# Four of the sixteen gates computed as two Strassen pairs inside the values' stage

## The chip, the core and the metric

The kernel runs on one core of a Trainium2 chip. The metric is the device time of one execution in microseconds (us). TensorE is called PE here, VectorE DVE, ScalarE ACT, GpSimd POOL and SyncE SP. Besides PE, an execution keeps DVE and ACT busy with element work, and SP and POOL with issuing transfers.

## What is computed

One decoder layer, batch 1, 1024 tokens, 1024 channels, float32. Only the first half matters here.

```
h   = rms_norm(x)
q,k,v (attention A: 4 heads, causal, two softmaxes), q,k,v (attention B: 3 dilated groups x 4 heads), 2 x 1024 gate columns = h @ w_in
yA  = DiffAttn(h) @ W_A_out ; yB = DilatedMix(h) @ W_B_out
x   = x + rms_norm((sigmoid(gA) * yA + sigmoid(gB) * yB) @ W_mix_out)
x   = x + rms_norm(ConvGLU(rms_norm(x)))
```

## The kernel before

**Matmuls in three products.** Every float32 operand is split into a rounded high half and the low rest (`whi`/`wlo`, `xh`/`xl`, and so on; `split`, lines 149 on ACT and 146 on DVE). `mm3` makes a product from three matmuls, high by high, high by low and low by high (lines 155, 156 and 157). A matmul with 512 moving columns is the unit in which most of the work comes.

**The values' stage.** After the start, all value columns of both attentions (4 blocks of 512 columns in two halves `i` = 0 and 1) are computed by Strassen's scheme: seven products `p1` to `p7` in place of eight, over sums of blocks of the normalized input (`t2`, `t3`, `t4` and the blocks `b11` to `b22`) and sums of blocks of the weight. The table `steps_v` names the product and the k block of each step, and the loop over it fetches raw weights ahead (SP's queue, `load_raw`), makes the weight sums on DVE (line 345, tiles `wz` and `raw`), splits them (`ready_v`, tiles `whi` and `wlo`), multiplies (`step_v`), and takes sums out of PSUM (`take_v`, `put_v`; tiles `yv` to DRAM `v_d`). Work on tables (`sin`, `cos`, `rstd_row`) stands among these steps on DVE and ACT by the step numbers `NORM_AT` to `STORE_AT`.

**Gates.** Sixteen blocks of 128 gate columns (`proj_t`, 48 matmuls of 512 columns each) give `gt_d` in DRAM. `START_GATES`, `A_FILLS` and `B_GATES` say where they stand: one before attention A, twelve spread as fills among the attention jobs of its heads, three in attention B's last step.

**Attention and its fills.** `interleave` writes out the order: attention jobs (scores `s`, softmax in `bs` and `stat`, transposes `pt`, product `o`, sum `osb`) with "fills" between them, projections and gates, so that PE has work while DVE and ACT do a job's softmax. In `A_FILLS` one string per head of attention A lists the fills: `p` projects the next head, `v` and `w` fetch and split values, `g` is a gate, `P` projects the first head of attention B, `x` and `V` fetch and split its values. In attention B each step's fills are the projections of the next step (`acc` is their PSUM tile, `kh`, `kl`, `qh`, `ql` what they become after the rotation, tiles `t1` and `t2`). The framework's scheduler then fixes each engine's order; how far the projections run ahead of the jobs follows from it. Each engine works through its own order in sequence. PSUM holds one `o` tile for the second attention's jobs, so a job's first product waits until `osb` has taken the previous one out (ACT line 1027 copies, DVE line 1028 adds).

**The last attention step and behind it.** Head 3 of the last group runs with the gates as fills and, behind them, the products of attention A's output (`oah`, `oal`). What its groups gave is stored (`og_d`, `st_d`), weighed, read back and summed (`merge`: DVE lines 1107 to 1110, tiles `mw`, `og`, `om`), split to `obh` and `obl`, and multiplied (`acc2`, `acc`).

Of the kernel before, what the change touches and what calls it, by code (L numbers as in the profile page):

```python
# [15 lines left out]
F32 = mybir.dt.float32  # L16
F32R = mybir.dt.float32r
I32 = mybir.dt.int32
AF = mybir.ActivationFunctionType
ALU = mybir.AluOpType  # L20
# [4 lines left out]
P = 128  # L25
S = 1024
D = 1024
KC = D // P
# [18 lines left out]
NH = NF // 2  # L47
AHEAD, T1_AT, LAST = 4, 5, 7
MIX_UNITS = {3: (0,), 4: (1,), 5: (2, 4), 6: (5,), 7: (6, 3, 7)}
START_GATES, A_FILLS, B_GATES = 1, ("gpgg", "gpvgg", "wgpgg", "xgPVgg"), 3  # L50
SLOTS = 18
LEFT_PAD = 48


XT_BUFS, NORM_AT, ANGLES_AT, SINES_AT, TABLES_AT, STORE_AT = 6, 14, 25, 33, 34, {35: 0, 36: 3, 39: 2, 41: 1}

K_FIRST = (4, 0, 5, 1, 6, 2, 7, 3)
RSQRT_MAGIC = float(0x5F3759DF)
# [29 lines left out]
def trunk(ctx: ExitStack, tc: tile.TileContext, a, out):  # L88
    nc = tc.nc
# [17 lines left out]
    def psum(dt=F32, pool=acc, tag="acc"):  # L107
        return pool.tile([P, 512], dt, tag=tag, name=tag)
# [8 lines left out]
    def load_raw(src, tag="raw", width=512, parts=1):  # L117
        raw = (raws_in[-1].tile([P, 512], F32, tag=tag, name="raw") if isinstance(tag, str) else tag)[:, :width]
        if src is None:
            return raw  # L120
        if parts > 1:
            for c in range(0, width, width // parts):
                dma(raw[:, c : c + width // parts], src[:, c : c + width // parts])
            return raw
        to = raw if src.dtype == F32 else raw.bitcast(I32)
        dma(to if len(src.shape) == 2 else to.rearrange("p (b c) -> p b c", c=src.shape[-1]), src)
        return raw
# [20 lines left out]
    def split(hi, lo, src, eng=None):  # L148
        copy = nc.scalar.activation(hi, src, AF.Copy)  # L149
        sub(eng or nc.vector, lo, src, hi)  # L150
        return copy.ins
# [48 lines left out]
    def halves():  # L200
        return [slice(i * 512, (i + 1) * 512) for i in range(2)]
# [142 lines left out]
    def tt(o, x, y, op=ALU.subtract):  # L344
        nc.vector.tensor_tensor(o, x, y, op=op)  # L345
# [82 lines left out]
    def turn_norms():  # L428
        spread = rstd_row.rearrange("p (m q) -> p m q", q=P)
        nc.vector.tensor_copy(spread, rstd.unsqueeze(2).to_broadcast([P, 8, P]))  # L430
        for half, sl in enumerate(halves()):
            row = psum(F32, ps_s, "s")
            for b in range(4):
                nc.tensor.transpose(row[:, b * P : (b + 1) * P], spread[:, half * 4 + b], ident)
            nc.scalar.activation(rstd_row[:, sl], row, AF.Copy)
# [25 lines left out]
    with ExitStack() as st_y:  # L461
# [6 lines left out]
        def turns(pattern, *ps):  # L468

            ks = [iter(range(4)) for _ in ps]  # L470
            return [(ps[c], 1, next(ks[c])) for c in pattern]

        steps_v += [("p1", 1, k) for k in range(4)] + turns((0, 0, 1, 0, 1, 0, 1, 1), "p5", "p6")
        steps_v += turns((0, 0, 1, 1, 1, 1, 0, 0), "p3", "p7") + [("p4", 1, k) for k in range(4)]
        wz = [t[:, k % 2] for t in [wv.tile([P, 2, 512], F32, tag=f"wz{i}", name="wz") for i in range(2)] for k in range(2)]
        ready, got_v = {}, {}
# [10 lines left out]
        def new_y(name, pool=None):  # L487
            return [(pool or yv).tile([P, 512], F32, tag=f"y{name}{m}", name="yv") for m in range(4)]

        def fetch_v(n):  # L490
            p, i, k = steps_v[n]
            which = {"p1": ((0, 0),), "p2": ((0, 1),), "p5": ((1, 0), (1, 1)), "p6": ((0, 0),), "p7": ((0, 0), (1, 0)),
                     "p4": ((1, 1),), "p3": ((0, 1),)}[p]
            got_v[n] = [load_raw(a["w_v"][j * 4 + k][:, (2 * i + c) * 512 : (2 * i + c + 1) * 512], next(tags), parts=1 if n else 2)
                        for c, j in which]

        def ready_v(n, w=512):
            p, _, k = steps_v[n]
# [54 lines left out]
        quarter = {(0, i): new_y(f"a{i}") for i in range(2)}  # L553
        banks = {}

        def step_v(n):
            p, i, k = steps_v[n]
            x = xs_of[p]
            if p in ("p1", "p2", "p5") and k == 0:
                left = p == "p1"  # L560
                banks[left] = ([psum() for _ in range(3)] + [psum(F32, ps_o, "o")] if left else
                               [psum(F32, q, t) for q, t in ((ps_s, "s"), (pt, "pt")) for _ in range(2)])
            use = banks[p in ("p1", "p6", "p7", "p4")]
            wh, wl = ready.pop(n)
            for m in range(4):
                tk = slice(m * P, (m + 1) * P)
                mm3(use[m], x[0][:, k, tk], x[1][:, k, tk], wh, wl, k == 0 and p in ("p1", "p2", "p5"), k == 3, p in ("p6", "p7", "p4", "p3"))
            if k < 3:
                return
            with tc.high_priority(offset=80):  # L570
                for m in range(4):
                    take_v(p, i, m, use[m])
            if p == "p7" and i == 0:
                for m in range(4):
                    tt(quarter[3, 0][m], banks[False][m], quarter[3, 0][m], ALU.add)
# [56 lines left out]
        for n in range(8, len(steps_v)):  # L632
            p, i, k = steps_v[n]
            while fetched < min(n + (8 if n <= TABLES_AT else 10), len(steps_v)):
                fetch_v(fetched)
                fetched += 1
            while made < min(n + 5, len(steps_v)):
                ready_v(made)
                made += 1
            if 0 <= n - NORM_AT < 11:  # L640
                norm_x(n - NORM_AT)
            if n == NORM_AT + 11:
                lambda_scale()
            if n == TABLES_AT + 2:
                scale_tables(*args)
            if n == TABLES_AT + 4:
                tags = more_tags()
            if n == ANGLES_AT:
                pos = [load_raw(a["positions"][sl].partition_broadcast(P), next(tags)) for sl in halves()]
                args = [tb.tile([P, S], F32, tag=n_, name=n_) for n_ in ("sin", "cos")]  # L650
                angles(pos, *args, tb)
            if n in STORE_AT:
                put_v(STORE_AT[n], 0, True)
            if n == SINES_AT:
                make_sines(*args)
            if n == TABLES_AT:
                turn_norms()
            if k == 0 and (p, i) in places_y:
                q, name, pool = places_y[p, i]
                quarter[q, i] = new_y(name, pool)  # L660
            step_v(n)
            if k == 3 and i and p in ("p1", "p7", "p4", "p3"):
                put_v({"p1": 0, "p7": 3, "p4": 2, "p3": 1}[p], 1, p == "p1")
            if (p, i) == ("p5", 1):

                again.append(load_raw(a["xT"][k][:, 512:], next(tags)))
            if (p, i) == ("p6", 1):
                with behind_marks():
                    split_x(k, halves()[1], again[k])
# [15 lines left out]
                dma(v.rearrange("p (r ih) c -> p r ih c", ih=n)[:, :, ih], src[:, i * 4 // n : (i + 1) * 4 // n, ih])  # L685
        return vs

    def split_values(vs, res):

        with behind_marks():  # L690
            for v in vs:
                res.append(v_tiles())
                split(*res[-1], v)

    def rotated(ps, cos, sin, sl, quarter):
        t1 = rt.tile([P, 512], F32, tag="t1", name="t1")
# [172 lines left out]
        later(1, sums)  # L869
        later(3, norm)  # L870

    free_gates = list(range(2 * KC))

    def gates(n):

# [32 lines left out]
    def once(fn):  # L908

        fn()  # L910
        yield 0
# [13 lines left out]
    with st_a:  # L925
        ops = [[] for _ in range(AH)]
        vs = [[] for _ in range(AH // 2)]
        run(gates(START_GATES)[0])
        run(proj_a(0, ops[0]))
        split_values(fetch_values(1, 0), vs[0])  # L930
        of_pair = []
        for h in range(AH):
            out_sb, pair = {}, []
            todo = [functools.partial(attend_a, h, i, ops[h], vs[h // 2], out_sb, pair) for i in (6, 7, 4, 5, 2, 3, 0, 1)]
            kinds = {
                "p": lambda: (proj_a(h + 1, ops[h + 1]), 8),
                "v": lambda: (once(lambda: of_pair.extend(fetch_values(1, 256))), 0),
                "w": lambda: (once(lambda: split_values(of_pair, vs[1])), 0),
                "g": lambda: gates(1),
                "P": lambda: (proj_b(0, 0, ops_b[steps[0]]), 8),  # L940
                "x": lambda: (once(lambda: fetch_b(0, 0)), 0),
                "V": lambda: (once(lambda: split_b(0, 0)), 0),
            }
            if h + 1 == AH:
                tabs_b += load_tabs(0, 64)
            fills = [kinds[c]() for c in A_FILLS[h]]
            if h + 1 < AH:
                interleave(jobs(todo, a_weight), 52, *fills)
            else:
                interleave(itertools.chain(jobs(todo, a_weight), rest_due(12)), 64, *fills)  # L950
# [516 lines left out]
    def put(step, *srcs):  # L1467

        operands[step] = []
        for src in srcs:  # L1470
            operands[step].append(next(places)())
            split(*operands[step][-1], src)
# [329 lines left out]
```

## Time and profile before

| | |
|---|---|
| median of 3 runs | 1685.25 us (1685.08 to 1686.24) |
| profiled execution | 1684.85 us, its span 1683.1 us |
| granted PE clock | 0.999 |
| PE busy | 1668.5 us, 99% of the span |
| DVE busy | 1308.4 us, 78% |
| ACT busy | 913.4 us, 54% |
| POOL busy | 170.2 us, 10% |

The span runs from the first to the last instruction; 1.75 us of the execution lie outside it. "Busy" of PE is the union of pipelined matmuls, so an individual duration of some 390 ns is not its cost: consecutive matmuls start 0.227 us apart. Which stage binds on what has to be read by windows of time and by the waits.

### The profile page before, as it was taken

The page shows a single profiled execution, that of the slowest core. Times are in us where ns is not written, and L with a number is a line of the kernel's source. Part 1 is how long each engine was busy: PE and PEld are TensorE (multiplying, and loading weights), DVE is VectorE, ACT ScalarE, POOL GpSimd, SP SyncE. Part 2 cuts the span into 40 slices and gives each one's busy share as a digit, 9 for nine tenths or more (in the row PEclk, how much of TensorE's full clock was granted, in tenths as well). Part 3 has the DMA queues.
Part 4 walks back from the last instruction along what each step waited for, and adds up shares of the span by engine and source line. Part 5 has one row for each costly group of instructions (what it writes and reads, how often), then busy time and mean ns, then how long its engine had stood idle before and what let it go on. Part 6 is the DMA issues. An engine that isn't in the chain of part 4 may idle for free. (4 is left out here: it accounts for less than half of the span.)

```text
span 1683.1 us, 22937 instructions
## 1 busy us (share of the span) xinstructions
PE 1668.5 (99%) x7878; PEld 1394.0 (83%) x7878; DVE 1308.4 (78%) x2430; ACT 913.4 (54%) x1707; POOL 170.2 (10%) x267
## 2 busy tenths in 40 slices
PE   9999999999999999999999999999999999999997
PEld 7888888888888888888888888887888888888886
DVE  8795576877777777788766865988888778799978
ACT  7633574655445677667554533565554455255453
POOL 0031000000000000000123400022211121000000
PEclk9999999999999999999999999999999999999999
DMA  8767421315122212343676532267755655296524
GB/s 269 234 221 266 132 83 62 107 57 147 48 70 75 76 57 78 107 135 105 212 264 223 188 113 89 58 159 172 161 133 132 156 137 126 96 348 214 193 88 150
DMA packets 117253, 241.59 MB, mean 144 GB/s; under 512 B 14528, under 2 KB 23680, under 8 KB 117136
## 3 DMA queue, kind: packets, MB, share of 16 engines
q1 hardware_dynamic: 89296, 171.28, 30.6%
q0 software_dynamic: 23088, 60.45, 15.2%
q10 hardware_dynamic: 4752, 8.39, 1.3%
q8 instruction: 62, 1.02, 0.3%
q14 instruction: 55, 0.45, 0.1%
HBM read 177.54 MB, written 47.86 MB: 134 GB/s over the span
## 5 line engine op out<-in xcount | busy, mean ns | idle before, releaser
L157 PE MATMUL acc<-xl,whi 128*128 128x512 f32 x768 | 302.5, 394 | 0.0
L155 PE MATMUL acc<-xh,whi 128*128 128x512 f32 x768 | 302.0, 393 | 0.0
L156 PE MATMUL acc<-xh,wlo 128*128 128x512 f32 x768 | 301.7, 393 | 0.0
L149 ACT ACTIVATE whi<-raw 128x512 fp32r<-128x512 f32 (+1 forms) x249 | 154.1, 627 | 180.6 <-PE acc L157 115.4
L146 DVE TENSOR_TENSOR wlo<-raw,whi 128x512 fp32r<-128x512 f32 (+1 forms) x249 | 172.2, 700 | 32.8 <-ACT whi L149 27.9
L156 PEld LDWEIGHTS acc<-xh,wlo 128*128 128x128 f32 x768 | 144.4, 188 | 27.9
L157 PEld LDWEIGHTS acc<-xl,whi 128*128 128x128 f32 x768 | 144.4, 188 | 27.7
L155 PEld LDWEIGHTS acc<-xh,whi 128*128 128x128 f32 x768 | 144.5, 188 | 27.3
L155 PE MATMUL acc<-mh,whi 128*128 128x512 f32 x384 | 149.7, 390 | 1.7 <-ACT u L1447 1.3
L156 PE MATMUL acc<-mh,wlo 128*128 128x512 f32 x384 | 149.4, 389 | 0.0
L157 PE MATMUL acc<-ml,whi 128*128 128x512 f32 x384 | 149.1, 389 | 0.0
L700 ACT ACTIVATE t<-acc 64x512 f32<-64x512 f32 (+1 forms) x160 | 94.7, 592 | 62.0 <-PE acc L157 60.4
L149 ACT ACTIVATE whi<-s 128x512 fp32r<-128x512 f32 x80 | 49.8, 627 | 90.7 <-PE acc L157 63.5
L1443 DVE TENSOR_TENSOR u<-acc,u 128x512 f32<-128x512 f32 x100 | 68.5, 687 | 29.1 <-PE acc L157 28.9
L701 DVE TENSOR_TENSOR t<-acc,cos 128x512 f32<-128x512 f32 x64 | 44.2, 690 | 55.4 <-ACT t L700 51.9
L155 PEld LDWEIGHTS acc<-mh,whi 128*128 128x128 f32 x384 | 72.1, 188 | 17.7 <-ACT u L1447 2.2
L157 PEld LDWEIGHTS acc<-ml,whi 128*128 128x128 f32 x384 | 72.1, 188 | 14.9
L156 PEld LDWEIGHTS acc<-mh,wlo 128*128 128x128 f32 x384 | 72.1, 188 | 14.9
L1620 PE MATMUL acc<-whi,wlo 128*128 128x512 f32 x216 | 76.1, 390 | 0.0
L1619 PE MATMUL acc<-whi 128*128 128x512 f32 x216 | 74.8, 389 | 0.0
L1621 PE MATMUL acc<-wlo,whi 128*128 128x512 f32 x216 | 71.6, 390 | 0.0
L787 DVE CUSTOM_DVE_ANT_0 s<-s,mask_a 128x512 f32<-128x512 f32 (+3 forms) x96 | 52.5, 555 | 23.2 <-PE s L785 18.5
(402 smaller groups left out, 4015.2 us busy)
## 6 DMA issues: line engine op xcount, KB each, us to landing
raw<-in_w_in SPq DMA_DIRECT2D x96, 256.0 KB, 2.8
raw<-in_w_v SPq DMA_DIRECT2D x71, 256.0 KB, 4.6
raw<-in_w_up SPq DMA_DIRECT2D x68, 256.0 KB, 3.6
raw<-c_d SPq DMA_DIRECT2D x48, 256.0 KB, 3.6
c_d<-c SPq DMA_DIRECT2D x22, 512.0 KB, 4.0
s<-in_w_up POOLq DMA_DIRECT2D x40, 256.0 KB, 4.2
s<-s POOLq DMA_DIRECT2D x40, 256.0 KB, 3.9
raw<-in_w_down SPq DMA_DIRECT2D x37, 256.0 KB, 3.5
```

The lines of the kernel that those rows point to most:

```text
L146: eng.tensor_tensor(lo, src, hi.bitcast(F32), op=ALU.subtract)
L149: copy = nc.scalar.activation(hi, src, AF.Copy)
L155: nc.tensor.matmul(o, sh, mh, start=first, stop=False, skip_group_check=on)
L156: nc.tensor.matmul(o, sl, mh, start=False, stop=False, skip_group_check=on)
L157: nc.tensor.matmul(o, sh, ml, start=False, stop=last, skip_group_check=on)
L700: nc.scalar.activation(t1[dst], ps[src], AF.Copy)
L701: nc.vector.tensor_tensor(t2, ps, cos[:, sl], op=ALU.mult)
L787: nc.vector.tensor_tensor_reduce(out=s_sb[:, c0:c1], in0=ps, in1=mask, scale=-scale, scalar=3.0e38, op0=ALU.add, op1=ALU.min, accum_out=mx ...
L1443: nc.vector.tensor_tensor(to, made(p), x, op=ALU.add)
L1619: nc.tensor.matmul(banks[m], gh[:, tk], wh, start=f == 0, stop=False)
L1620: nc.tensor.matmul(banks[m], gl[:, tk], wh, start=False, stop=False)
L1621: nc.tensor.matmul(banks[m], gh[:, tk], wl, start=False, stop=f == NH - 1)
```

## The change

Two pairs of gate blocks, four of the sixteen (`gate_of`: the last ones), are computed in the values' stage by the same seven products: the steps `(p, "gate", x)` stand between the second half's `p1` and `p5`. Each such step is four products of `mm3`, 12 matmuls; a pair takes 84 matmuls in place of 96. Their weight sums and splits go through `fetch_v` and `ready_v`, their sums out of PSUM through `take_gate`, and the results go to `gt_d` by POOL's queue. The first three heads of attention A lose one gate each, and attention B's last step goes from three to two; head 3 keeps three. The `w` fill splits the second value pair in pieces of two blocks rather than four. `STORE_AT` moves the stores of the first half's values.

```diff
-START_GATES, A_FILLS, B_GATES = 1, ("gpgg", "gpvgg", "wgpgg", "xgPVgg"), 3
+PAIRS, START_GATES, A_FILLS, B_GATES = 2, 1, ("gpg", "gpvg", "wgpg", "xgPVgg"), 2
...
-..., STORE_AT = 6, 14, 25, 33, 34, {35: 0, 36: 3, 39: 2, 41: 1}
+..., STORE_AT = 6, 14, 25, 33, 34, {32: 0, 37: 3, 42: 2, 46: 1}
...
+        steps_v += [(p, "gate", x) for p in ("p2", "p1", "p5", "p6", "p7", "p4", "p3") for x in range(PAIRS)]
...
+            if i == "gate":
+                srcs = [w_in[where[GT + gate_of(k, c) * P]][:, j * 512 : (j + 1) * 512] for c, j in which]
...
+        def take_gate(p, n, use):
+            def put(q):
+                sl = halves()[q % 2]
+                y = gate_y[n][q]
+                tt(y, use if p == "p4" else y, rstd_row[:, sl], ALU.mult)
+                nc.gpsimd.dma_start(gt_d[gate_of(n, q // 2)][:, sl], y)
+            y = gate_y[n]
+            if p in ("p2", "p6", "p7"):
+                nc.scalar.activation(y[{"p2": 0, "p6": 1, "p7": 3}[p]], use, AF.Copy)
+            if p == "p1":
+                tt(y[0], use, y[0], ALU.add)
+                put(0)
...
+        def step_gate(p, n, wh, wl):
+            left = p in ("p1", "p6", "p7", "p4")
+            if p in ("p1", "p2"):
+                banks[n, left] = psum(F32, pt, "pt") if left else psum(F32, ps_s, "s")
+            x, use = xs_of[p], banks[n, left]
+            for k in range(4):
+                c = slice(k * P, (k + 1) * P)
+                mm3(use, wh[:, c], wl[:, c], x[0][:, k], x[1][:, k], k == 0 and p in ("p1", "p2", "p5"), k == 3, p in ("p6", "p7", "p4", "p3"))
...
+                for b in range(0, 4, parts):
+                    split(*(t[:, b : b + parts] for t in (*res[-1], v)))
...
-    free_gates = list(range(2 * KC))
+    free_gates = list(range(2 * (KC - PAIRS)))
...
-                "w": lambda: (once(lambda: split_values(of_pair, vs[1])), 0),
+                "w": lambda: (once(lambda: split_values(of_pair, vs[1], 2)), 0),
```

The lines of the changed kernel have numbers 52 higher from the values' stage on (1027 becomes 1079, 895 becomes 947).

**First place: PE at the first jobs of attention B.** Each of attention B's steps has four jobs for one head. Before, where the first step's fourth job gives its product (`o_5377`) and the third step's scores (`s_5629`) are made, a projection follows at once:

```order
L727 MATMUL o_5377<-pt_5310,vl_4828 128x128 x2
L727 MATMUL o_5377<-pt_5310,vl_4828 128x256
L713 MATMUL pt_5458<-ident_76,bs_5422 128x128
L713 MATMUL pt_5541<-ident_76,bs_5488 128x128 x4
L155 MATMUL s_5629<-kh_5350,qh_5348 128x256
L156 MATMUL s_5629<-kh_5350,ql_5349 128x256
L157 MATMUL s_5629<-kl_5351,qh_5348 128x256
L155 MATMUL acc_5797<-xh_98,whi_5785 128x512
L156 MATMUL acc_5797<-xh_98,wlo_5786 128x512
L157 MATMUL acc_5797<-xl_99,whi_5785 128x512
L155 MATMUL acc_5797<-xh_98,whi_5785 128x512
```

The projections `acc_5797` and `acc_5845` go on from there with 26 matmuls before the next job's product, `o_5434`, the second step's first. In the changed kernel the products of the same two jobs are `o_5480` and `o_5537`, and the third step's scores begin with `s_5732` and `s_5811`:

```order
L779 MATMUL o_5480<-pt_5413,vl_4931 128x128 x2
L779 MATMUL o_5480<-pt_5413,vl_4931 128x256
L765 MATMUL pt_5561<-ident_76,bs_5525 128x128 x4
L765 MATMUL pt_5644<-ident_76,bs_5591 128x128 x4
L777 MATMUL o_5537<-pt_5500,vh_4926 128x512
L777 MATMUL o_5537<-pt_5500,vh_4926 128x2x128
L779 MATMUL o_5537<-pt_5500,vl_4927 128x128
L779 MATMUL o_5537<-pt_5500,vl_4927 128x256
L765 MATMUL pt_5707<-ident_76,bs_5681 128x128 x4
L155 MATMUL s_5732<-kh_5453,qh_5451 128x128
L156 MATMUL s_5732<-kh_5453,ql_5452 128x128
L155 MATMUL s_5811<-kh_5453,qh_5451 128x128
```

Nine more score matmuls follow these rows and then `acc_5948`. Between `o_5480` and `acc_5948` there is no projection, where there were 26 of its matmuls and more before; the projections stand earlier in PE's order.

**Second place: ACT at the same jobs.** Before, the splits of the next value pair (`vh`) and of the keys (`kh`) stand ahead of the copy of the first step's third product (`osb_5058<-o_5290`):

```order
L149 ACTIVATE vh_5493<-vperm_5328 128x1024
L149 ACTIVATE vh_5497<-vperm_5329 128x1024
L700 ACTIVATE t1_5699<-acc_5657 64x512 x2
L895 ACTIVATE kh_5350<-t2_5556 128x4x128
L895 ACTIVATE kh_5350<-t2_5619 128x4x128
L1027 ACTIVATE osb_5058<-o_5290 128x256
L149 ACTIVATE pt_5397<-pt_5393 128x384
L1051 ACTIVATE rows_5448<-pt_5447 16x128
```

In the changed kernel they stand behind that copy, which is `osb_5161<-o_5393` there, and among the copies and softmaxes that follow:

```order
L1079 ACTIVATE osb_5161<-o_5393 128x256
L149 ACTIVATE pt_5500<-pt_5496 128x384
L1103 ACTIVATE rows_5551<-pt_5550 16x128
L1051 ACTIVATE bs_5591,stat_5438<-bs_5591,stat_5438 128x256 x2
L149 ACTIVATE vh_5596<-vperm_5431 128x1024
L1079 ACTIVATE osb_5161<-o_5480 128x256
L149 ACTIVATE pt_5566<-pt_5561 128x512
L1051 ACTIVATE bs_5681,stat_5438<-bs_5681,stat_5438 128x256
L149 ACTIVATE vh_5600<-vperm_5432 128x1024
L1051 ACTIVATE bs_5681,stat_5438<-bs_5681,stat_5438 128x256
L947 ACTIVATE kh_5453<-t2_5659 128x4x128
L947 ACTIVATE kh_5453<-t2_5722 128x4x128
```

The scores `s_5732` on PE read both halves of `kh_5453`, and `acc_5948` takes the PSUM buffer of `acc_5760`, which DVE frees by `t2_5803<-acc_5760,cos` behind both `kl_5454`.

**Third place: DVE at the inserted gates.** Before, in the values' second half, DVE's order in the middle of the table work is

```order
L345 TENSOR_TENSOR wz_135<-raw_1175,wz_135 128x512
L345 TENSOR_TENSOR raw_1222<-raw_1222,raw_1224 128x512
L146 TENSOR_TENSOR wlo_1251<-wz_136,whi_1250 128x512
L383 SCALAR_TENSOR_TENSOR xl_99<-raw_1220,edge_58,xh_98 128x512
L345 TENSOR_TENSOR sin_899<-sin_899,rstd_row_112 128x512 x2
L146 TENSOR_TENSOR wlo_1278<-wz_136,whi_1277 128x512
L146 TENSOR_TENSOR wlo_1308<-wz_135,whi_1307 128x512
L146 TENSOR_TENSOR wlo_1329<-wz_135,whi_1328 128x512
```

and in the changed kernel, where the gates' products `p1` to `p6` stand,

```order
L345 TENSOR_TENSOR yv_1189<-pt_1269,yv_1189 128x512
L345 TENSOR_TENSOR yv_1188<-yv_1188,rstd_row_112 128x512
L146 TENSOR_TENSOR wlo_1266<-wz_135,whi_1265 128x512
L146 TENSOR_TENSOR wlo_1289<-raw_1137,whi_1288 128x512
L146 TENSOR_TENSOR wlo_1309<-raw_1169,whi_1308 128x512
L146 TENSOR_TENSOR wlo_1329<-raw_1210,whi_1328 128x512
L345 TENSOR_TENSOR wz_135<-raw_1262,wz_135 128x512
L345 TENSOR_TENSOR yv_1189<-yv_1189,rstd_row_112 128x512
L345 TENSOR_TENSOR wz_135<-raw_1285,wz_135 128x512
L146 TENSOR_TENSOR wlo_1355<-raw_1239,whi_1354 128x512
```

The weight sums into `wz` and the products with `rstd_row` for the gates (`yv_1188`, `yv_1189`) stand between the splits that PE waits for.

More of the change, by code (lines that the diff above doesn't have):

```diff
@@ L49 @@
 MIX_UNITS = {3: (0,), 4: (1,), 5: (2, 4), 6: (5,), 7: (6, 3, 7)}
-START_GATES, A_FILLS, B_GATES = 1, ("gpgg", "gpvgg", "wgpgg", "xgPVgg"), 3
+PAIRS, START_GATES, A_FILLS, B_GATES = 2, 1, ("gpg", "gpvg", "wgpg", "xgPVgg"), 2
 SLOTS = 18
 LEFT_PAD = 48
-XT_BUFS, NORM_AT, ANGLES_AT, SINES_AT, TABLES_AT, STORE_AT = 6, 14, 25, 33, 34, {35: 0, 36: 3, 39: 2, 41: 1}
+XT_BUFS, NORM_AT, ANGLES_AT, SINES_AT, TABLES_AT, STORE_AT = 6, 14, 25, 33, 34, {32: 0, 37: 3, 42: 2, 46: 1}
 K_FIRST = (4, 0, 5, 1, 6, 2, 7, 3)
@@ L471, in turns @@
             return [(ps[c], 1, next(ks[c])) for c in pattern]
-        steps_v += [("p1", 1, k) for k in range(4)] + turns((0, 0, 1, 0, 1, 0, 1, 1), "p5", "p6")
+        steps_v += [("p1", 1, k) for k in range(4)]
+        steps_v += [(p, "gate", x) for p in ("p2", "p1", "p5", "p6", "p7", "p4", "p3") for x in range(PAIRS)]
+        steps_v += turns((0, 0, 1, 0, 1, 0, 1, 1), "p5", "p6")
         steps_v += turns((0, 0, 1, 1, 1, 1, 0, 0), "p3", "p7") + [("p4", 1, k) for k in range(4)]
@@ L488, in new_y, with gate_of @@
             return [(pool or yv).tile([P, 512], F32, tag=f"y{name}{m}", name="yv") for m in range(4)]
+        def gate_of(x, c):
+            return 2 * (KC - PAIRS + x) + c
         def fetch_v(n):
@@ L493, in fetch_v @@
                      "p4": ((1, 1),), "p3": ((0, 1),)}[p]
-            got_v[n] = [load_raw(a["w_v"][j * 4 + k][:, (2 * i + c) * 512 : (2 * i + c + 1) * 512], next(tags), parts=1 if n else 2)
-                        for c, j in which]
+            if i == "gate":
+                srcs = [w_in[where[GT + gate_of(k, c) * P]][:, j * 512 : (j + 1) * 512] for c, j in which]
+            else:
+                srcs = [a["w_v"][j * 4 + k][:, (2 * i + c) * 512 : (2 * i + c + 1) * 512] for c, j in which]
+            got_v[n] = [load_raw(src, next(tags), parts=1 if n else 2) for src in srcs]
         def ready_v(n, w=512):
@@ L554, in trunk @@
         banks = {}
+        gate_y = {}
+        def take_gate(p, n, use):
[10 more added lines that the diff above has]
+                put(0)
+            if p == "p7":
+                tt(y[3], banks[n, False], y[3], ALU.add)
+                put(3)
+            if p == "p4":
+                put(2)
+            if p == "p3":
+                tt(y[1], use, y[1], ALU.add)
+                put(1)
+        def step_gate(p, n, wh, wl):
[6 more added lines that the diff above has]
+                mm3(use, wh[:, c], wl[:, c], x[0][:, k], x[1][:, k], k == 0 and p in ("p1", "p2", "p5"), k == 3, p in ("p6", "p7", "p4", "p3"))
+            with tc.high_priority(offset=80):
+                take_gate(p, n, use)
         def step_v(n):
             p, i, k = steps_v[n]
+            if i == "gate":
+                step_gate(p, k, *ready.pop(n))
+                return
             x = xs_of[p]
@@ L657, in trunk @@
                 turn_norms()
+            if (p, i, k) == ("p2", "gate", 0):
+                ya, yb = new_y("a0"), new_y("b3", yw)
+                gate_y.update({x: {0: ya[x], 1: ya[2 + x], 3: yb[x], 2: yb[2 + x]} for x in range(PAIRS)})
             if k == 0 and (p, i) in places_y:
@@ L686, in fetch_values, with split_values @@
         return vs
-    def split_values(vs, res):
+    def split_values(vs, res, parts=4):
         with behind_marks():
@@ L692, in split_values @@
                 res.append(v_tiles())
-                split(*res[-1], v)
+                for b in range(0, 4, parts):
+                    split(*(t[:, b : b + parts] for t in (*res[-1], v)))
     def rotated(ps, cos, sin, sl, quarter):
```

## The prediction

> **What bounds the kernel now.** I read the page's shares first, then PE's waits, then windows of time.
>
> ```profile
> PE 1668.5 (99%) x7878; PEld 1394.0 (83%) x7878; DVE 1308.4 (78%) x2430; ACT 913.4 (54%) x1707; POOL 170.2 (10%) x267
> ```
>
> ```profile
> PE acc L155 <- ACT xh L387: 1.4, 1, 1.4
> PE acc L155 <- DVE ya L1211: 1.4, 2, 0.9
> PE acc L155 <- ACT u L1447: 1.3, 1, 1.3
> PE pt L594 <- DVE t4l L591: 1.2, 1, 1.2
> ```
>
> PE sets the time, and its waits come to a few us in all. Matmuls taken away are therefore worth their own time, unless PE begins to wait for something that it does not wait for now. In the windows (PE, PEld, DVE, ACT, POOL busy, clock, DMA share, GB/s) the reader is to see how much DVE and ACT do under a full PE:
>
> ```profile
> 80.00:100.00 20.00, 20.00 (x90) 16.57 (x89) 20.00 (x39) 8.76 (x13) 0.00 (x0) 1.00 0.47 138
> 100.00:120.00 20.00, 20.00 (x94) 16.63 (x93) 19.67 (x40) 6.02 (x9) 11.46 (x14) 1.00 0.68 234
> 120.00:140.00 20.00, 20.00 (x90) 16.54 (x90) 13.68 (x23) 9.42 (x16) 5.04 (x9) 1.00 0.99 357
> 540.00:560.00 20.00, 20.00 (x120) 17.73 (x119) 13.16 (x36) 14.09 (x35) 0.00 (x0) 1.00 0.13 40
> 560.00:580.00 20.00, 20.00 (x112) 17.34 (x111) 18.23 (x37) 16.00 (x34) 0.00 (x0) 1.00 0.32 107
> 860.00:870.00 10.00, 9.13 (x42) 7.24 (x42) 7.46 (x11) 4.05 (x6) 2.41 (x4) 1.00 0.81 290
> 1670.00:1684.00 14.00, 4.35 (x20) 3.27 (x18) 8.91 (x21) 1.86 (x6) 0.00 (x0) 0.82 0.52 197
> ```
>
> The first two attention B steps are the tight place: in 560 to 580 DVE works 18.23 and ACT 16.00 of 20 us, and PE stays full only because projections stand between the jobs.
>
> **Removed: 24 matmuls.** Two pairs cost 2 x 84 matmuls where four gates cost 4 x 48 = 192.
>
> ```profile
> 127.75 0.39 PE L155 MATMUL o<-whi,t2h 128*128 128x512 f32 x1
> ...
> 131.38 0.39 PE L156 MATMUL pt<-whi,xl 128*128 128x512 f32 x1
> ```
>
> These two are the first and the last of 17 consecutive starts of 512-column matmuls: 3.63 / 16 = 0.227 us each. 24 x 0.227 = 5.44 us, all on the engine that sets the time: **-5.44**. Moving the other 168 matmuls forward costs PE nothing in itself.
>
> **Added in the values' stage: DVE sums, copies and splits.** Per pair four weight sums, seven splits, three sums out of PSUM and four products with `rstd_row`, 18 operations of 512 elements at 0.60 us each (from the starts of `cos` to `sin`, 590.65 to 591.26, in a fence below): 36 x 0.60 = 21.6 us against 168 x 0.227 = 38.1 us of new PE work. The rate is no problem; the entry is, because DVE comes in with 20.00 and 19.67 of 20 us used and the gates stand in its order among the table work. DVE is 57% loaded by the gates themselves, so it drains its backlog at 0.43 us per us. Ahead of the products `p6` I count DVE's rows through to about 1.2 us before PE's need. The extra loads, ten of 256 KB, go into a stretch where DMA runs at 0.99 in 120 to 140:
>
> ```profile
> raw<-in_w_v SPq DMA_DIRECT2D x71, 256.0 KB, 4.6
> ```
>
> A load that comes late is waited for by a weight sum on DVE, with the next split behind it and PE behind that; one load more in the way is 4.6 us against a margin of 1.2, so the bounds are 0 and 3.4. PE was full there with DVE at 20.00, so I take **+0.3**, near the lower end. The gates' stores go to POOL's queue, behind value stores; POOL is 11.46 of 20 busy in its fullest window and nobody in this stage reads `gt_d`: 0. The `w` pieces cost an ACT and a DVE start more; the values are fetched a head before their use: 0.
>
> **Heads 0 to 2 without one gate each.** 10.9 us less PE work (48 x 0.227) stands over the same softmaxes. Attention A still has its other fills, and the nearest score-to-transpose distance keeps about 8 us of PE work against a softmax of a few: 0.
>
> **Attention B's first jobs.** Here the orders show what changed for a wait: 26 projection matmuls (5.9 us) that stood between the first step's last product and the second's first are gone from there, and 3.9 us of small matmuls are all that PE has from the third product's end (`o_5393`) to `acc_5948`. Their prices:
>
> ```profile
> 575.65 0.57 PE L725 MATMUL o<-pt,vh 128*128 128x512 f32 x2
> 576.29 0.60 PE L713 MATMUL pt<-ident,bs 128*128 128x128 f32 x4
> 576.78 0.33 PE L155 MATMUL s<-kh,qh 128*128 128x256 f32 x1
> 577.19 0.22 PE L155 MATMUL s<-kh,qh 128*128 128x128 f32 x1
> 577.47 0.33 PE L155 MATMUL s<-kh,qh 128*128 128x256 f32 x1
> 581.52 0.62 PE L725 MATMUL o<-pt,vh 128*128 128x512 f32 x3
> 582.33 0.49 PE L713 MATMUL pt<-ident,bs 128*128 128x128 f32 x3
> 582.57 0.30 PE L155 MATMUL s<-kh,qh 128*128 128x128 f32 x1
> ```
>
> From start to start: `o_5480` 0.81 (581.52 to 582.33), `o_5537` 0.64 (575.65 to 576.29), 13 transposes at 0.08 (582.33 to 582.57 is three) 1.04, two jobs' scores at 0.69 (576.78 to 577.47) 1.38. Sum 3.9 us.
>
> ACT has in the same stretch, in the order shown: `osb`, `pt` 384, `rows`, two exponentials, `vh`, `osb`, `pt` 512, one exponential, `vh`, one exponential, `kh`, `kh`. Nothing of this can start before `o_5393` is done, as its copy stands first. The prices, again from start to start:
>
> ```profile
> 538.37 0.49 ACT L999 ACTIVATE bs<-bs,stat 128x256 f32<-128x256 f32 x1
> 538.86 0.50 ACT L999 ACTIVATE bs<-bs,stat 128x256 f32<-128x256 f32 x1
> 558.25 2.00 ACT L149 ACTIVATE vh<-vperm 128x1024 fp32r<-128x1024 f32 x2
> 561.49 2.13 ACT L895 ACTIVATE kh<-t 128x512 fp32r<-128x512 f32 x2
> 563.52 0.37 ACT L1027 ACTIVATE osb<-o 128x256 f32<-128x256 f32 x1
> 563.79 0.49 ACT L149 ACTIVATE pt<-pt 128x384 fp32r<-128x384 f32 x1
> 564.16 0.25 ACT L1051 ACTIVATE rows<-pt 16x128 f32<-16x128 f32 x1
> 564.32 0.61 ACT L149 ACTIVATE whi<-raw 128x512 fp32r<-128x512 f32 x1
> 576.77 0.59 ACT L149 ACTIVATE pt<-pt 128x512 fp32r<-128x512 f32 x1
> 577.24 1.14 ACT L895 ACTIVATE kh<-t 128x512 fp32r<-128x512 f32 x1
> ```
>
> 0.27 + 0.37 + 0.16 + 4 x 0.49 + 2.00 + 0.27 + 0.47 + 2.13 = 7.6 us until both `kh` are there. DVE then makes the second `kl` and frees `acc_5760`:
>
> ```profile
> 578.57 1.07 DVE L896 TENSOR_TENSOR kl<-t,kh 128x512 fp32r<-128x512 f32 x1
> 590.65 0.69 DVE L701 TENSOR_TENSOR t<-acc,cos 128x512 f32<-128x512 f32 x1 [1.57 <-ACT t L700]
> 591.26 0.68 DVE L702 TENSOR_TENSOR t<-t,sin 128x512 f32<-128x512 f32 x1
> ```
>
> 1.07 + 0.69 = 1.8, so `acc_5948` can begin 9.4 us after `o_5393`, and PE has 3.9 us of work: it waits 5.5 us, in pieces at `o_5537`, at the scores and at `acc_5948`. DVE's own rows up to there are about as long and do not add. Bounds: without the last hop and with `kl` half hidden 4 us; with both of the next value pair's low halves (1.2 us each on DVE) ahead of `kl` in the way 8 us. I take **+5.5**, the sum of the rows. The cover of these splits now is the projections, and it is that which goes.
>
> **The last step with two gates.** The last head's sums go out, are read back merged, and are due at `obh`. The present chain, from the last product:
>
> ```profile
> 873.87 0.22 PE L727 MATMUL o<-pt,vl 128*128 128x128 f32 x1
> ...
> 879.87 0.65 DVE L1028 TENSOR_TENSOR osb<-osb,o 128x256 f32<-128x256 f32 x1
> ...
> 891.85 1.76 DVE L1107 TENSOR_TENSOR mw<-og,mw 128x1536 f32<-128x1536 f32 x1 [5.12 <-DMA mw<-e_d]
> ...
> 897.31 0.69 DVE L146 TENSOR_TENSOR obl<-om,obh 128x512 fp32r<-128x512 f32 x1
> ```
>
> It takes 23.4 us from the last product to the split, 17.4 of them behind the last `osb` sum. A gate fewer behind the last job leaves 10.9 us less PE work, but products of `obh`'s other heads stand before the need, some 19 us by PE's rows. The 1.4 us that PE already waits for `ya` (line 1211, blocked behind line 1107) may go or stay. Bounds -1.4 and +4; I take **+0.2**.
>
> **Sum.** 1684.85 - 5.44 + 0.3 + 5.5 + 0.2 = 1685.4 for the profiled execution, which lies 0.4 below the median of 1685.25; against the runs I forecast **1685.5**. A change of 0.2% (3.4 us, 1681.9 to 1688.6) is about what a measurement of this kernel can tell from none.
>
> **Rivals.**
> *The gain comes through.* If PE enters attention B's jobs late enough for ACT to be ahead, or DVE and ACT overlap better than in sequence, the bare stretch costs under 2 us: 1679.9 to 1681.9. For it: PE waited nowhere between 40 and 860 us. Against: ACT's copy of `o_5393` cannot be ahead of PE.
> *The clock falls.* In 1670 to 1684, where PE works 4.35 of 14 us, the granted clock is 0.82; after waits of 0.9 us, in 860 to 870, it is 1.00. A loss of 0.18 over 14 us is 2.5 us at most, so 1688. [...] Against it: the wait is broken by small matmuls.
> *The last merge is late.* This one ends slower. If the chain keeps its 23.4 us and PE has 19 us, PE waits 4.4 us: 1685.5 + 4.4 = 1689.9. It decides from 3.1 us on. For it: DVE waits 5.12 us for `e_d` there. Against: some of the chain is DVE's queue, which is shorter with a gate less.
>
> **Chances.** The forecast 0.58 (1682 to 1688.5), the full gain 0.17, the clock 0.05, the late merge 0.12, a late load in the values' stage 0.08 (up to 3.4 more, 1688.9). Faster is the second, 0.17; slower takes the merge, most of the late load and a part of the clock, 0.21; the same 0.62. The range 1681.5 to 1690 leaves out most of the full gain and the far end of the merge.
>
> **What the changed profile would show.** PE with 24 fewer 512-column matmuls; new waits of PE at `o`, `s` and `acc` on ACT `kh` and DVE's line 948 or 753 of some 5 us within 20 us of attention B's start; none in attention A. If PE's busy column stays at 20.00 there, the forecast is wrong and the time is near 1680. A wait of `pt` or `s` on `wlo` between 105 and 145 shows the values' stage, more than 1.4 us at `ya`, or a wait at `acc2`, the merge.

## The result, and the profile after

The changed kernel takes 1707.0 us (median of 4 runs, 1705.5 to 1709.0) against 1685.2 before (4 runs, 1684.9 to 1686.2): a ratio of 1.0131, 95% interval [1.0116, 1.0146], 22 us slower. The forecast was 1685.5. The profiled execution spans 1706.0 us against 1683.1.

The waits of PE tell most of it (us in total, times, longest):

```profile
PE s L836 <- DVE mx L839: 4.4, 3, 2.0
PE acc L155 <- ACT obh L149: 3.0, 2, 2.6
PE acc L155 <- DVE gl L1295: 2.8, 1, 2.8
PE o L777 <- DVE osb L1080: 2.7, 2, 1.9
...
PE pt L155 <- ACT yv L576: 2.3, 1, 2.3
PE acc L155 <- DVE ya L1263: 1.9, 1, 1.9
...
PE s L155 <- ACT kh L947: 0.5, 1, 0.5
PE o L777 <- DVE pt L146: 0.3, 1, 0.3
```

Apart from waits of the start (`xh` and `t4l`; 2.6 us of them stood there before) and 0.7 us behind 960 us, they lie in four places: the inserted products (`yv`, at 129 us), attention A at the step from head 1 to head 2 (`mx`, 405 to 413), attention B's first jobs (`osb`, `kh`, 589 to 595), and the last merge and the mixing behind it (`ya`, `obh`, `gl`, 888 to 938). Small windows show a second loss, in the clock (columns PE, PEld, DVE, ACT, POOL busy, then the granted PE clock):

```profile
405.00:410.00 5.00, 2.65 (x11) 1.38 (x10) 5.00 (x12) 3.87 (x8) 1.03 (x2) 1.00 0.17 37
410.00:415.00 5.00, 2.49 (x8) 1.77 (x9) 4.88 (x12) 0.63 (x1) 1.03 (x2) 0.55 0.54 124
415.00:420.00 5.00, 5.00 (x15) 4.13 (x16) 4.67 (x18) 4.34 (x9) 0.00 (x0) 0.50 0.71 181
420.00:425.00 5.00, 5.00 (x27) 4.15 (x25) 4.84 (x11) 1.58 (x3) 0.00 (x0) 0.93 0.73 230
```

In 415 to 420 PE is busy all the time and does 15 matmuls, where 22 of 512 columns fit at the full clock (5.00 us at the 0.227 us between two starts). The other two places look the same:

```profile
592.00:595.00 3.00, 1.36 (x8) 1.06 (x8) 3.00 (x6) 3.00 (x7) 0.00 (x0) 0.97 0.23 93
595.00:598.00 3.00, 2.60 (x11) 2.42 (x12) 2.85 (x5) 2.10 (x4) 0.00 (x0) 0.50 0.23 87
598.00:601.00 3.00, 3.00 (x10) 2.42 (x10) 3.00 (x12) 0.77 (x1) 0.00 (x0) 0.50 0.00 0
601.00:604.00 3.00, 3.00 (x13) 2.47 (x12) 3.00 (x6) 2.94 (x10) 0.00 (x0) 0.89 0.00 0
```

```profile
890.00:895.00 5.00, 4.68 (x16) 3.92 (x17) 4.82 (x13) 3.61 (x7) 2.83 (x5) 0.68 0.71 238
...
935.00:940.00 5.00, 2.16 (x9) 1.52 (x8) 5.00 (x9) 4.20 (x7) 1.81 (x2) 0.96 0.65 202
940.00:945.00 5.00, 5.00 (x17) 3.95 (x17) 5.00 (x6) 3.93 (x8) 4.13 (x3) 0.70 0.31 112
```

What the clock cost I estimate as PE's busy time in a window times the missing share of the clock (2.49 x 0.45 + 5.00 x 0.50 + 5.00 x 0.07 = 4.0 in the first fence):

| place | PE waits, us | lost by the clock, us |
|---|---|---|
| values' stage, 129 | 2.3 | 0 |
| attention A, 405 to 425 | 4.8 | 4.0 |
| attention B's first jobs, 589 to 604 | 3.2 | 3.2 |
| last merge, 888 to 945 | 7.7 (before 1.4) | 3.2 |

18.0 - 1.4 of waits and 10.4 of clock, less the 5.44 of 24 matmuls, make 21.6 of the 22.9 us between the spans; the remaining 1.3 I don't assign. The kernel before shows no clock below 1.00 in these stages.

### The profile page after: what moved, and what is told of

Same layout as the page of the kernel before. It is cut to its first block, busy times and chain, and to the rows that moved or that the text cites. A ratio compares the mean times of both kernels' runs of the same rounds, so it can differ in the third digit from the quotient of the medians.

```text
span 1706.0 us, 22954 instructions
## 1 busy us (share of the span) xinstructions
PE 1674.8 (98%) x7854; PEld 1396.0 (82%) x7854; DVE 1322.4 (78%) x2452; ACT 919.9 (54%) x1721; POOL 172.9 (10%) x275
## 5 line engine op out<-in xcount | busy, mean ns | idle before, releaser
L156 PE MATMUL acc<-xh,wlo 128*128 128x512 f32 x704 | 278.7, 396 | 0.0
L155 PE MATMUL acc<-xh,whi 128*128 128x512 f32 x704 | 278.5, 396 | 0.0
L157 PE MATMUL acc<-xl,whi 128*128 128x512 f32 x704 | 277.9, 395 | 0.0
L155 PEld LDWEIGHTS acc<-xh,whi 128*128 128x128 f32 x704 | 133.4, 189 | 25.7
L156 PEld LDWEIGHTS acc<-xh,wlo 128*128 128x128 f32 x704 | 133.4, 189 | 25.7
L157 PEld LDWEIGHTS acc<-xl,whi 128*128 128x128 f32 x704 | 133.3, 189 | 25.7
L846 ACT ACTIVATE s<-s,mx 128x896 f32<-128x896 f32 (+7 forms) x64 | 49.3, 772 | 34.0 <-DVE mx L843 20.0
```

The lines of the kernel that those rows point to most:

```text
L155: nc.tensor.matmul(o, sh, mh, start=first, stop=False, skip_group_check=on)
L156: nc.tensor.matmul(o, sl, mh, start=False, stop=False, skip_group_check=on)
L157: nc.tensor.matmul(o, sh, ml, start=False, stop=last, skip_group_check=on)
L846: exp = nc.scalar.activation(sc[c][:, :w], sc[c][:, :w], AF.Exp, bias=mx[:, c, 0:1], scale=-1.0, accum_out=den[:, c : c + 1])
```

## The experiments

The theory: PE's work in the four gates was cover. Where it is gone, attention and merge show their own latency on PE, and the clock falls after. The rival: the inserted products, with their loads, stores and sums, upset the stages behind them. Every edit below also lets the scheduler write a new order, so what is compared is more or less work to fill with, not one order with rows taken out. Each ratio is to the kernel before as it was measured beside that version (1684.3 us, and 1683.8 in the last three).

### The same thin fills without the inserted products

```diff
-PAIRS, START_GATES, ... = 2, 1, ("gpg", "gpvg", "wgpg", "xgPVgg"), 2
+PAIRS, START_GATES, ... = 0, 5, ("gpg", "gpvg", "wgpg", "xgPVgg"), 2
```

`STORE_AT` is that of before.

> No gate pair in the values' stage (PAIRS 0); four gates stand ahead of attention A instead (START_GATES 5), and the thinner fills of the change stay (2, 2, 2, 3 gates in the heads, 2 in the last step). Theory, lost cover: PE waits at the same three places as in the changed kernel (attention A near 405 us, attention B's first jobs near 590, the last merge near 890 to 940), only the 2.3 us wait in the values' stage goes and 24 matmuls (5.4 us) come back: about 1710 us. Rival, the inserted products upset the stages behind them through late loads, stores and a shifted order: without them the waits go and the time is about 1685 to 1688.

Measured: 1709.4 us (1705.3 to 1709.5), ratio 1.014 [1.0124, 1.0156]. PE waits at the same three places, and not on `yv`. In attention A and in the merge the waits are the same ones; attention B's first jobs wait 4.7 us here, on `kl`, `stat`, `rows` and `osb`. The clock falls at all three.

```profile
PE s L836 <- DVE mx L839: 4.5, 3, 2.1
PE acc L155 <- ACT obh L149: 2.7, 2, 2.4
PE acc L155 <- DVE gl L1295: 2.7, 1, 2.7
```

So the Strassen products aren't needed for the loss behind the values' stage: taking four gates out of the attention fills is enough.

### The gates back, place by place

Heads 0 to 2 with three gates, head 3 with none:

```diff
-... = 2, 1, ("gpg", "gpvg", "wgpg", "xgPVgg"), 2
+... = 2, 1, ("gpgg", "gpvgg", "wgpgg", "xPV"), 2
```

> The pairs stay; heads 0 to 2 keep three gates each as before, and head 3 has none (its fills are x, P, V). Theory, lost cover: the wait of attention A near 405 us with its half clock goes (-9.9 us), the last merge stays (9.7 us), attention B's first jobs cost as much or more than in the changed kernel (6.6 us): 1695 to 1705. Rival, the inserted products upset the stages behind them: the wait near 405 us stays and the time is 1705 or more.

Measured: 1699.1 us (1698.2 to 1703.4), ratio 1.0093 [1.0074, 1.0112]. PE waits nowhere between 380 and 460 us, but head 3 and attention B's first jobs wait in its place, and the clock falls at head 3 (it stays at 1.00 at attention B's first jobs). The last merge waits and loses clock as in the changed kernel.

```profile
PE acc L155 <- DVE t L753: 3.2, 1, 3.2
PE s L155 <- ACT kh L947: 1.8, 1, 1.8
PE o L777 <- DVE osb L1080: 1.2, 1, 1.2
```

```profile
535.00:540.00 5.00, 3.25 (x8) 2.58 (x9) 4.77 (x15) 1.94 (x4) 0.00 (x0) 0.69 0.01 3
```

The last step with three gates, none ahead of attention A:

```diff
-... = 2, 1, ("gpg", "gpvg", "wgpg", "xgPVgg"), 2
+... = 2, 0, ("gpg", "gpvg", "wgpg", "xgPVgg"), 3
```

> The pairs stay; the last step has three gates again, and the gate ahead of attention A goes instead (START_GATES 0). Theory, lost cover: the waits near 890 to 940 us and their low clock go back to the 1.4 us of before (7.7 + 3.4 - 1.4 = 9.7 us less), the two other places stay: about 1697. Rival, the merge's transfers are what is late, whatever stands beside them: 1705 to 1707.

Measured: 1703.9 us (1699.6 to 1705.4), ratio 1.0109 [1.0091, 1.0126]. The profiled execution, which is the fastest one, spans 1697.7 us. Behind 860 us this is left of the waits:

```profile
PE acc L155 <- DVE ya L1263: 2.4, 2, 1.3
PE o L777 <- DVE osb L1080: 0.7, 1, 0.7
```

The waits on `obh` and `gl` are gone, and with them the low clock; the two other places stand as they were. So the traced execution bears the theory out. The median doesn't: it lies nearer to the rival's 1705 than to 1697. The other three executions took 4 to 6 us longer than the traced one, and what they waited for isn't shown; their mean clock was 0.992 against 0.994, by an estimate from the two figures (0.002 of 1700 us) some 3 us more lost to the clock.

Both at once:

```diff
-... = 2, 1, ("gpg", "gpvg", "wgpg", "xgPVgg"), 2
+... = 2, 0, ("gpgg", "gpvgg", "wgpgg", "xPV"), 3
```

> The pairs stay; heads 0 to 2 have three gates each, the last step three, head 3 and the place ahead of attention A none. Theory, lost cover: the places near 405 and near 890 to 940 us go, what is left is the values' stage (2.3 us) and attention B's first jobs (6.6 us or more, as head 3's fills are fewer): 1685.2 - 5.4 + 2.3 + 6.6 = 1689, up to 1695. If head 3's gates are no cover for attention B's first jobs, 1682 to 1689. Rival, the inserted products upset the stages behind them: 1700 or more.

Measured: 1696.1 us (1693.2 to 1697.8), ratio 1.0065 [1.0049, 1.0081], a little above the expected 1689 to 1695. It is the best of the versions with two pairs and still slower than before: head 3's missing gates cost a wait of 3.2 us on `t` (line 753), attention B's first jobs 3.1, the merge 2.3 and the inserted products 2.5, each but the last with a fall of the clock.

### Was it the pieces of the value split?

```diff
-                "w": lambda: (once(lambda: split_values(of_pair, vs[1], 2)), 0),
+                "w": lambda: (once(lambda: split_values(of_pair, vs[1])), 0),
```

> As the changed kernel, but the second value pair is split whole (4 blocks at a time, as before) and not in pieces. Theory, lost cover: the four pieces of DVE near 405 us are the same work as two whole ones, so attention A's wait there stays within 2 us of its 4.8 us and the clock falls there as well: 1705 to 1709. Rival, the pieces cause that wait, since they stand between the maxima on which PE waits: about 1697.

Measured: 1704.6 us (1703.4 to 1708.3), ratio 1.0128 [1.0113, 1.0143]. Attention A waits 4.2 us on `mx` in place of 4.4, its longest wait is 3.1 in place of 2.0, and the clock falls to 0.66. The pieces aren't the cause.

### Matmuls that compute nothing

If cover is what was lost, plain PE work must do as well as a gate. A fill of matmuls on resident operands, whose result nobody reads:

```diff
+    def blank(n):
+        ps = psum()
+        for k in range(n):
+            nc.tensor.matmul(ps, xh[:, 0, :P], xh[:, 0, :512], start=True, stop=True)
+            if k % 6 == 5:
+                yield 0.5
...
+                "d": lambda: (blank(24), 2),
...
-... = 2, 1, ("gpg", "gpvg", "wgpg", "xgPVgg"), 2
+... = 2, 1, ("gpg", "gpvgd", "wgpg", "xgPVgg"), 2
...
-    interleave(jobs(todo), 4, gates(B_GATES))
+    interleave(jobs(todo), 4, gates(B_GATES), (blank(24), 2))
```

> As the changed kernel, with 24 matmuls more in head 1 and 24 more in the last step, on operands that lie in SBUF, whose result nobody reads: 10.9 us of work for PE alone, none for DVE, ACT or DMA. Theory, lost cover and clock: the wait near 405 us falls to 1 or 2 us and the clock stays at 1.00 there (some -8 us), the last merge's waits and its low clock go (-8 to -10 us), attention B's first jobs stay: 1707 + 10.9 - 17 = 1701, less time with more work. Rival, a gate was needed there for what DVE, ACT or the queues do in it, or the waits are fixed by transfers: 1710 to 1718.

Measured: 1699.1 us (1698.7 to 1699.6), ratio 1.0092 [1.0077, 1.0107]: 7 to 8 us less than the changed kernel (6.6 by the ratios, 7.9 by the medians), with 48 matmuls (10.9 us) more. Attention A waits 1.2 us in all, and the same stretch runs at the full clock:

```profile
410.00:415.00 5.00, 3.88 (x20) 2.91 (x19) 4.94 (x12) 1.36 (x3) 1.03 (x2) 1.00 0.91 202
415.00:420.00 5.00, 5.00 (x27) 4.22 (x26) 3.90 (x11) 4.41 (x9) 0.00 (x0) 1.00 1.03 241
```

In the last step 1.3 us of waits are left, none on `obh` or `gl`, with the clock at 1.00. Attention B's first jobs, where nothing was added, wait 4.7 us.

With 48 such matmuls for each of the four gates taken away:

```diff
-... = 2, 1, ("gpg", "gpvg", "wgpg", "xgPVgg"), 2
+... = 2, 1, ("gpgd", "gpvgd", "wgpgd", "xgPVgg"), 2
...
+                "d": lambda: (blank(48), 4),
...
-    interleave(jobs(todo), 4, gates(B_GATES))
+    interleave(jobs(todo), 4, gates(B_GATES), (blank(48), 4))
```

> As the changed kernel, with 48 such matmuls in place of each of the four gates that the change took away (heads 0, 1 and 2, last step). Theory, lost cover: all waits of PE behind the values' stage are those of before and the clock is 1.00, so the time is before + 168 matmuls of 0.227 us (38.1) + the values' stage's wait (2.3): 1684.3 + 40.4 = 1725. That prices the inserted products by themselves. Rival, the inserted products upset the stages behind them: 1735 or more, with waits at the three places.

Measured: 1725.4 us (1723.0 to 1728.0), ratio 1.0253 [1.0236, 1.027], against 1725 expected. Of PE's waits between 140 and 980 us a single one is left, as before the change:

```profile
PE acc L155 <- DVE ya L1271: 1.5, 1, 1.5
```

Its clock is 1.00 in every window up to 1700 us. The median is 41.6 us above the kernel before that was measured beside it (1683.8), where the 168 matmuls make 38.1 and the values' stage's wait 0.8 in the profile; 2.7 us stay open, within the spread of the runs. So the inserted products cost their matmuls and at most some 3 us more, and the loss behind them goes once PE has other work there.

## Why the prediction was wrong

**The matmuls, -5.44: right.** PE has 7854 matmuls in place of 7878, and the last experiment adds up to within 3 us.

**Values' stage, +0.3 (bounds 0 and 3.4): the size was low, the late load as written, the path another one.** I had the load awaited by a weight sum on DVE. In the trace a raw load of a gate was late, ACT stood at its split with the copy out of PSUM behind it, and PE behind that:

```profile
130.03 0.63 ACT L149 ACTIVATE whi<-raw 128x512 fp32r<-128x512 f32 x1 [7.58 <-DMA raw<-in_w_in]
130.57 0.58 ACT L576 ACTIVATE yv<-pt 128x512 f32<-128x512 f32 x1
```

```profile
raw<-in_w_v SPq DMA_DIRECT2D x9, 256.0 KB, 8.4
raw<-in_w_in SPq DMA_DIRECT2D x2, 256.0 KB, 8.3
```

PE waited 2.3 us. The load's price was taken from the median of the whole kernel, 4.6 us; between 115 and 131 us, with a DMA share of 1.03, the values' loads take 8.4 us and the gates' 8.3 from issue to landing. The trace before had this to read: 9.7 us for its five loads of `in_w_v` in the same window. And the ten loads more that I counted are the difference over the whole kernel; the pairs bring 18 into this stage.

**Heads 0 to 2 at 0: the step that failed first.** It measured 8.8 us (4.8 of wait, 4.0 of clock). I held the distance from scores to transposes, about 8 us of PE work, against one softmax. What failed is that overlap: the 8 us of PE work weren't there. PE comes to a stretch without any matmul of a projection or a gate (`acc`), between these two:

```profile
404.35 0.39 PE L157 MATMUL acc<-xl,whi 128*128 128x512 f32 x1
...
415.89 0.77 PE L155 MATMUL acc<-xh,whi 128*128 128x512 f32 x1
```

That is 11.5 us; at attention B's first jobs it is 16.3 (582.12 to 598.38). In the kernel before no such stretch between 200 and 660 us is longer than 2.8 us. I had looked for one in the orders of attention B's first jobs alone, and had named "none in attention A" among the signs. What PE waits for in the stretch is the buffer of the scores, which DVE's maximum (line 839) frees (4.4 us in the first fence), and DVE is full with three kinds of work:

```profile
407.96 1.29 DVE L146 TENSOR_TENSOR vl<-vperm,vh 128x512 fp32r<-128x512 f32 x2
409.17 0.68 DVE L803 TENSOR_TENSOR b<-t,a 64x512 fp32r<-64x512 f32 x1
409.77 0.68 DVE L839 CUSTOM_DVE_ANT_0 s<-s,mask_a 128x512 f32<-128x512 f32 x1
...
410.49 2.13 DVE L803 TENSOR_TENSOR b<-t,a 64x512 fp32r<-64x512 f32 x3
```

Those are the next value pair's low halves, the next head's rotated operands, and then the maximum. DVE is busy 5.00 and 4.88 of 5 us there, while its mean in 220 to 340 us of the trace before is 77% (46.76 and 46.12 of 60 us): the mean hid a place where the next head's operands and the values come due together. My sum over queue order, which I made for attention B, was not made here.

**Attention B's first jobs, +5.5: right in the chain, short by the clock.** From `o_5393` to `acc_5948` I had 9.4 us. In the trace `o_5393` ends at 588.75 (the first row, 588.25 + 0.50) and `acc_5948` starts at 598.38: 9.6 us.

```profile
588.25 0.50 PE L779 MATMUL o<-pt,vl 128*128 128x128 f32 x3
589.68 0.73 PE L777 MATMUL o<-pt,vh 128*128 128x512 f32 x3 [0.82 <-DVE osb L1080]
...
593.54 0.62 PE L777 MATMUL o<-pt,vh 128*128 128x512 f32 x2 [1.90 <-DVE osb L1080]
...
598.38 0.63 PE L155 MATMUL acc<-xh,whi 128*128 128x512 f32 x1
```

```profile
594.20 2.15 ACT L947 ACTIVATE kh<-t 128x512 fp32r<-128x512 f32 x2
...
597.40 0.68 DVE L753 TENSOR_TENSOR t<-acc,cos 128x512 f32<-128x512 f32 x1
```

Both `kh` are there at 596.35, 7.6 us behind `o_5393` as summed, and DVE frees `acc_5760` at 598.08. Of the 5.5 us, 3.2 show as waits. The wait that I had at `acc_5948` doesn't: PE, busy at half clock, comes to it only as it is freed. About 1.6 us of half clock follow behind 598.38.

**The last merge, +0.2: undersized.** It measured 9.5 us (7.7 - 1.4 of waits, 3.2 of clock). The rival had it at 4.4 us with a chance of 0.12; its mechanism, a chain longer than PE's work, is the one seen, but its 23.4 us ended at the wrong split. The merge makes `obh` and `obl` in four pieces; 897.31 is the third, and the fourth stands at 908.26 in the trace before, 34.4 us behind the last product. In the changed kernel the last product is at 901.50, and PE waits for the fourth piece:

```profile
933.62 0.69 DVE L146 TENSOR_TENSOR obl<-om,obh 128x512 fp32r<-128x512 f32 x1 [0.69 <-ACT obh L149]
```

```profile
933.64 0.50 PE L155 MATMUL acc<-obh,whi 128*128 128x512 f32 x1 [2.64 <-ACT obh L149]
```

That is 32.1 us: the chain is no longer than before, PE's work beside it is less. DVE stands in line 1159 for what is read back:

```profile
DVE mw L1159 <- DMA og<-og_d: 11.7, 2, 6.5
DVE mw L1159 <- DMA mw<-e_d: 7.0, 1, 7.0
```

Before, DVE's waits for `og` and `mw` there came to 2.6 and 8.5 us. PE has a gate less to pass the time while the sums go out and come back. Behind `obh` the mixing's first product waits as well (`gl`, 2.8 us), which no step of mine had.

**The clock: a rival with a chance of 0.05 and 2.5 us.** It cost 10.4 us, at three places, and comes on top of the forecast, not in its stead. I took its size from a mean of 0.82 over 14 us, of which most lie behind PE's last matmul: in 1670 to 1675 the trace before has 1.00, in 1675 to 1680 0.90 and in 1680 to 1684 0.50, the last two with PE idle. And I had held against it that small matmuls break the wait: 6 to 11 matmuls stand in each of the four stretches ahead of the falls (the fence below), and the clock fell all the same. Windows of 1 us of the changed kernel put the clock at half from 410.5 to 420.7, 594.8 to 601.6, 891.8 to 895.2 and 939.6 to 943.0 us: three, two, one and one times 3.41 us. The later starts lie 184.3, 481.3 and 529.1 us behind the first, 54, 141 and 155 times 3.413 us, so the falls stand on a grid that doesn't begin with a wait. These are the two stretches of the grid at 129 us, which no fall follows, and then those ahead of the four falls:

```profile
127.19:130.61 3.42, 1.75 (x8) 1.13 (x6) 0.85 (x2) 0.58 (x2) 0.54 (x1) 1.00 1.04 357
130.61:134.02 3.41, 2.82 (x12) 2.34 (x13) 2.68 (x4) 2.07 (x5) 0.00 (x0) 1.00 1.00 363
407.09:410.50 3.41, 1.49 (x8) 0.95 (x7) 3.38 (x9) 1.80 (x4) 1.03 (x2) 1.00 0.39 80
591.41:594.82 3.41, 1.51 (x11) 1.06 (x8) 3.41 (x8) 3.41 (x9) 0.00 (x0) 1.00 0.14 58
888.37:891.78 3.41, 1.50 (x7) 1.24 (x7) 3.33 (x7) 2.83 (x4) 1.33 (x2) 1.00 0.17 16
936.15:939.57 3.42, 1.42 (x6) 1.20 (x7) 3.42 (x6) 2.62 (x5) 1.38 (x2) 1.00 0.84 259
```

PE is busy in 42 to 44% of the stretches ahead of the falls, and in 51 and 83% of the two that share the wait at 129. Each fall of one stretch cost 1.7 us, by an estimate from the windows (half of 3.41 us, from 891.8 and from 939.6 on); the other two lasted three and two stretches.

## What to carry to other kernels

Where one engine is full and the others wait for it, its work is also the cover of their latency: before taking matmuls away, ask of each place what else would have to be done there in time, by each engine's own order and not by its mean load. In the orders, look for a stretch of the full engine without any of its large work, at every place where jobs change and not only where one suspects it. A gain of a few us on the bound engine is lost at the first place where the chain behind it is longer than what is left (here 5.44 us against 8.8 us in attention A alone). A short stall costs more than its length where the clock falls after it (4.8 us of waits and 4.0 us by the clock at 405 to 425 us; 2.3 us and none at 129), so the price of lost cover was stall plus half-speed work.

## What the runs showed of the hardware

Between 60 and 960 us of the changed kernel PE's granted clock falls to 0.50 four times, for three, two, one and one times 3.41 us, on a grid of such stretches, and PE is busy in 42 to 44% of the stretch ahead of each fall. A wait of 1.9 us at 888, within one stretch, stood ahead of a fall; one of 2.3 us at 129, spread over two, didn't bring one.

Six traces have such falls between 60 and 960 us, 17 in all: that of the changed kernel four, of the same thin fills three, of the gates back in heads 0 to 2 two, of the last step with three gates two, of both at once three, of the value split whole three. In windows of 5 us, PE is busy 1.80 to 3.41 of 5 us at each of the 17, in the window in which the clock first falls or in the one ahead. In five other windows, of four traces, it is busy 2.87 to 3.52 us and no fall comes. How the chip counts a busy PE wasn't tried. 48 matmuls whose results nobody reads, 10.9 us of work, made the kernel 7 to 8 us faster.
